# A dilated convolution: the fifth pair's load in two parts, and a small copy ahead of the first store

## The chip, the core and the metric

The kernel runs on one core of a Trainium2 chip. The metric is the device time of one execution in microseconds (us); the kernel before takes 126.56 us (median of 3 runs, 126.45 to 127.11).

The core's engines each run their own instruction stream: TensorE (PE) multiplies, VectorE (DVE), ScalarE (ACT) and GpSimd (POOL) work element by element, and SyncE (SP) issues transfers. Transfers themselves are carried out by 16 DMA engines, which take work from two queues here: SyncE's (f32 to f32) and GpSimd's (which also turns f32 into f16 on the way).

## The reference

```python
batch, c_in, h, w, c_out, k, dilation = 16, 64, 64, 64, 128, 3, 2
x_pad = np.pad(x, ((0, 0), (0, 0), (pad, pad), (pad, pad)), mode='constant')
for b in range(batch):
    for co in range(c_out):
        for ci in range(c_in):
            for kh in range(k):
                for kw in range(k):
                    output[b, co] += weight[co, ci, kh, kw] * x_pad[b, ci, kh*dilation:kh*dilation+h, kw*dilation:kw*dilation+w]
```

A 3 x 3 convolution with dilation 2, 64 channels to 128, on 16 images of 64 x 64, in f32. The input has 16.8 MB, the output 33.6 MB.

## The kernel before

Two images make a pair: their 2 x 64 input channels fill the 128 partitions. There are eight pairs (`NP`), counted pb = 0 to 7, and for each one

- a load of 128 partitions x 4096 values, f32 in memory and f16 in the tile `x16[pb]`. Pair 0 is loaded as f32 by SyncE (line 75) into a buffer of the output pool and converted on the chip; pairs 1 to 7 are loaded by GpSimd (line 81, and line 89 for the last one, which is cut unevenly);
- a sum on GpSimd (`prepare`, line 151): within each group of four rows the first two rows plus the last two, in the tile `s16[pb]`. With it, three products take the place of four;
- four units of 16 output rows (`NU`), each with three phases of matmuls into PSUM (line 196). The first phase works on `s16` and is copied out by ScalarE (line 217); the two others work on `x16`, and VectorE adds that copy to each (line 222) and writes the output tile `o`;
- a store from `o` to memory by SyncE (lines 233 to 237): one DMA of 4 MB for pairs 0 to 4, two of 2 MB for pairs 5 and 6 (pairs from `BOTH` = 5 on go image by image), and four of 1 MB for pair 7.

The order of the work is the order of the code; nothing is moved by a scheduler. Each engine takes its instructions in that order and waits by semaphores where it needs another's result. What matters around the change:

- GpSimd, at the start: the load of pair 1 (line 120), the first piece of pair 0's sum (line 155), the loads of pairs 2, 3 and 4 one right after another (lines 156 and 157, `AHEAD` = 5), and three more pieces of pair 0's sum (lines 158 and 159). Later loads are issued two pairs ahead, from within the loop (lines 205 to 209): pair 5's in pair 3's place of GpSimd's stream, and so on. DMAs of GpSimd's queue are worked off in order on each DMA engine.
- SyncE, at the start: the weight (line 64) and pair 0 in two pieces (line 75). After that it does nothing but the 13 stores, each waiting for VectorE to have finished its tile. A store that waits holds up all behind it on SyncE.
- Output tiles: `opool` has three buffers. `x32`, the f32 copy of pair 0, takes the first, so the tiles of pairs 0, 1, 2 are in the second, third and first one; pair 3 writes where pair 0's tile was and has to wait until that is stored, pair 4 waits for pair 1's, and so on.
- `x16pool` has six buffers, so the loads of pairs 1 to 5 wait for no buffer. `sumpool` has three: pair 4's sum takes the buffer of pair 1's.

Of the kernel before, what the change touches and what calls it, by code (L numbers as in the profile page):

```python
# [10 lines left out]
def kernel(  # L11
# [7 lines left out]
    nc = tc.nc  # L19

    B, CI, H, W = x.shape
# [5 lines left out]
    P = 128  # L27
    f32 = mybir.dt.float32
    f16 = mybir.dt.float16
    NP = B // 2  # L30
# [18 lines left out]
    wpool = ctx.enter_context(tc.tile_pool(name="wpool", bufs=1))  # L49
    x16pool = ctx.enter_context(tc.tile_pool(name="x16pool", bufs=6))  # L50
# [9 lines left out]
    x_pair = x.rearrange("(nb two) c h w -> nb (two c) h w", two=2)  # L60
# [5 lines left out]
    x16 = {}  # L66
# [11 lines left out]
    def load(pb, cuts):  # L78
        x16[pb] = x16pool.tile([P, H, W], f16, tag="x16", name=f"x16_{pb}")
        for lo, hi in zip(cuts, cuts[1:]):  # L80
            nc.gpsimd.dma_start(out=x16[pb][:, lo:hi], in_=x_pair[pb, :, lo:hi])  # L81

    def load_uneven(pb):
        x16[pb] = x16pool.tile([P, H, W], f16, tag="x16", name=f"x16_{pb}")
        cut, p1 = H - 36, P - 16
        parts = [(0, p1, 0, H), (p1, P, 0, cut)]
        parts += [(p, p + 4, cut, H) for p in range(p1, P, 4)]
        for p0, p2, lo, hi in parts:
            nc.gpsimd.dma_start(  # L89
                out=x16[pb][p0:p2, lo:hi], in_=x_pair[pb, p0:p2, lo:hi]  # L90
            )

    AHEAD = 5
# [16 lines left out]
    for name, a in (("w21", 2), ("w01", 0)):  # L110
        for u in range(2):
            eng = nc.vector if name == "w21" else nc.gpsimd
            eng.tensor_sub(  # L113
                out=w16[:, SLOT[name] * KW : (SLOT[name] + 1) * KW, u, :],
# [8 lines left out]
    for n, name in enumerate(("w1", "w21", "w0", "w01", "w2")):  # L123
        ps = cpool.tile([P, 2, NB], f32, tag="ps", name=f"wt{n}")
        k0 = SLOT[name] * KW
        for j in range(KW):
            nc.tensor.matmul(  # L127
                out=ps[:, 0, j * CO : (j + 1) * CO],
# [16 lines left out]
    def prepare(pb, lo, hi):  # L145
        if pb not in s16:
            s16[pb] = sumpool.tile([P, 2 * NQ, W], f16, tag="s16", name=f"s16_{pb}")
        src = (x16[pb] if pb else x32).rearrange("p (q e r) w -> p q e (r w)", e=2, r=2)
        dst = s16[pb].rearrange("p (q r) w -> p q (r w)", r=2)
        q0, q1 = lo // 4, hi // 4  # L150
        nc.gpsimd.tensor_add(  # L151
            out=dst[:, q0:q1], in0=src[:, q0:q1, 0, :], in1=src[:, q0:q1, 1, :]
        )

    prepare(0, 0, 20)
    for pb in range(2, AHEAD):
        load(pb, [0, H])
    for lo, hi in zip(cuts0[1:], cuts0[2:]):
        prepare(0, lo, hi)

# [30 lines left out]
    def phase(pb, u, terms):  # L191

        ps = cpool.tile([CO, 2, NB], f32, tag="ps", name="ps")
        for pair in zip(*(conv(pb, hb, ps[:, hb], u, terms) for hb in range(2))):
            for m in pair:
                nc.tensor.matmul(**m)  # L196
        return ps

    BOTH = NP - 3
    for pb in range(NP):  # L200
        o = opool.tile([P, 2, H, W], f32, tag="o", name=f"o{pb}")
        ov = o.rearrange("p b (q e r) w -> p b q e (r w)", e=2, r=2)
        for u in range(NU):

            if u == 1 and AHEAD <= pb + 2 < NP:
                if pb + 3 == NP:
                    load_uneven(pb + 2)
                else:
                    load(pb + 2, [0, H])
            if pb + 1 < NP:  # L210
                if u == 1:
                    prepare(pb + 1, 0, 36 if pb + 1 < 3 else H)
                elif u == 2 and pb + 1 < 3:
                    prepare(pb + 1, 36, H)

            s32 = spool.tile([P, 2, NB], f32, tag="s32", name="s32")
            nc.scalar.copy(out=s32, in_=phase(pb, u, [("w1", 2, 0)]))  # L217
            for e, terms in enumerate(
                ([("w21", 1, 0), ("w0", 1, -1)], [("w01", 0, 0), ("w2", 0, 1)])
            ):  # L220
                ps = phase(pb, u, terms)
                nc.vector.tensor_add(  # L222
                    out=ov[:, :, u * UQ : (u + 1) * UQ, e, :],
                    in0=ps.rearrange("p b (q c) -> p b q c", c=QW),
                    in1=s32.rearrange("p b (q c) -> p b q c", c=QW),
                )

            step = NU // 2 if pb == NP - 1 else NU  # L230
            if (u + 1) % step == 0:
                fl = slice((u + 1 - step) * 4 * UQ, (u + 1) * 4 * UQ)
                if pb < BOTH:
                    nc.sync.dma_start(out=out_pair[pb], in_=o)
                else:
                    for hb in range(2):
                        nc.sync.dma_start(out=out[2 * pb + hb, :, fl], in_=o[:, hb, fl])
# [35 lines left out]
```

## Time and profile before

| | |
|---|---|
| time, median of 3 runs | 126.56 us (126.45 to 127.11) |
| the profiled execution | 126.83 us, of which the span from the first to the last instruction is 125.1 us |
| granted TensorE clock | 0.965 of full speed, mean of the span |
| TensorE busy | 104.8 us (84% of the span) |
| VectorE busy | 81.9 us (66%) |
| GpSimd busy | 43.0 us (34%) |
| ScalarE busy | 39.6 us (32%) |
| SyncE's DMA queue (weight, pair 0, all stores) | 35.95 MB, 68.4% of the time of 16 DMA engines |
| GpSimd's DMA queue (loads of pairs 1 to 7) | 7.34 MB as written, 28.9% |

The two queues' shares of DMA time add up to 97.3%. A load of GpSimd's queue reads twice the bytes that it writes, and the profile counts those written.

The stores, by their issue on SyncE: 23.43 us (pair 0), 35.80 (pair 1), 48.17 (pair 2), 60.54 (pair 3), 75.59 (pair 4), 87.97 (the first of pair 5) and so on to 113.08 (the last). The five stores of 4 MB take 24.3 us from issue to landing (median), the four of 2 MB 12.5 us; the six loads of 1 MB (as written) 15.3 us.

How to read what the prediction shows: times are microseconds from the start of the span. A row of the timeline has the start, the duration, the engine, the line of the kernel, the operation with the tiles that it writes and reads, the count, and in brackets the engine's idle time before it and what ended that. "SPq" is SyncE's issuing of a DMA, not the transfer. In the rows of "slices" the span is cut into 40 equal parts of 3.13 us; the digit of the DMA row is the busy share of the 16 DMA engines in tenths (9 is 90% or more).

### The profile page before, as it was taken

What the parts mean: (1) busy time and instruction counts of PE and PEld (TensorE: products, weight loads), DVE (VectorE), ACT (ScalarE), POOL (GpSimd) and SP (SyncE); (2) the same over time, 40 slices, a digit from 0 to 9 for tenths busy, and PEclk for the clock granted to TensorE, in tenths of its full rate; (3) what the DMA queues carried; (4) which work ended last, traced back from release to release, by engine and by line L of the source; (5) the groups of instructions that cost most, each with busy time, mean ns of one, the idle gap of its engine ahead of it and who ended that gap; (6) DMA issues with size and microseconds to landing.
All of it is one profiled execution on the core that took longest, in us unless ns stands there. A gap on an engine that the chain in (4) does not pass through costs nothing.

```text
span 125.1 us, 2248 instructions
## 1 busy us (share of the span) xinstructions
PE 104.8 (84%) x981; PEld 56.0 (45%) x981; DVE 81.9 (66%) x71; ACT 39.6 (32%) x40; POOL 43.0 (34%) x33
## 2 busy tenths in 40 slices
PE   6379999999999999999947999999999999960000
PEld 2055555555555555555524555555555555520000
DVE  0484877877787778777319978777877787770000
ACT  4777333333333333333330333333332433310000
POOL 2789696993580079507500093000000000000000
PEclk9999999999999999999999999999999999999655
DMA  4999999999999999999999999999999999999991
GB/s 138 368 332 210 212 215 220 220 170 367 375 330 309 343 299 333 335 301 333 330 420 410 422 435 435 424 440 419 419 425 445 430 422 435 425 417 409 432 406 76
DMA packets 4105, 43.42 MB, mean 347 GB/s; under 512 B 496, under 2 KB 496, under 8 KB 784
## 3 DMA queue, kind: packets, MB, share of 16 engines
q1 hardware_dynamic: 2944, 35.95, 68.4%
q0 software_dynamic: 1152, 7.34, 28.9%
q8 instruction: 7, 0.11, 0.3%
q14 instruction: 2, 0.02, 0.0%
HBM read 17.07 MB, written 33.55 MB: 405 GB/s over the span
## 4 chain that ended last, share of the span: by engine, by line
PE 55%; DMA 28%; DVE 4%; POOL 1%; DVEq 1%; issue 0%; SPq 0%
PE ps L196 55%; DMA out_dram<-o 24%; DMA x<-in_x_dram 5%; DVE o L222 4%; POOL s L151 1%; DVEq L268 1%; SPq L64 0%; DVEq L222 0%
## 5 line engine op out<-in xcount | busy, mean ns | idle before, releaser
L222 DVE TENSOR_TENSOR o<-ps,s 128x1024 f32<-128x1024 f32 x64 | 76.7, 1222 | 25.9 <-PE ps L196 17.1
L196 PE MATMUL ps<-x,w_sb 64*128 64x496 f16 (+3 forms) x768 | 84.9, 366 | 2.5 <-DVE o L222 2.5
L196 PEld LDWEIGHTS <-w_sb 64*128 64x128 f16 x960 | 53.7, 94 | 49.6 <-issue 4.8
L217 ACT COPY s<-ps 128x1024 f32<-128x1024 f32 x32 | 32.4, 1012 | 66.9 <-PE ps L196 66.9
L151 POOL TENSOR_TENSOR s<-x 128x2048 f16<-128x2048 f16 (+5 forms) x13 | 33.8, 2616 | 30.0 <-PE ps L196 23.6
L196 PE MATMUL ps<-s,w_sb 64*128 64x496 f16 (+1 forms) x192 | 26.6, 379 | 0.7 <-POOL s L151 0.7
L81 POOL DMA_DIRECT2D x<-in_x_dram x6 | 3.8, 634 | 0.0
L103 PE MATMUL warm<-zero 128*128 128x512 f16 x6 | 2.7, 630 | 1.2 <-DVE zero L97 1.2
L127 PE MATMUL wt<-ident,w 128*128 128x128 f16 x15 | 1.8, 312 | 2.1 <-ACT w L109 2.1
L113 DVE TENSOR_TENSOR w<-w 128x192 f16<-128x192 f32 x2 | 1.5, 796 | 2.5 <-DMA w<-in_weight_dram 2.5
L89 POOL DMA_DIRECT2D x<-in_x_dram x6 | 3.1, 522 | 0.0
L127 PEld LDWEIGHTS <-w 128*128 128x128 f16 x15 | 1.5, 145 | 3.1 <-ACT w L109 3.1
L109 ACT CAST w<-w 128x576 f16<-128x576 f32 x2 | 2.3, 1222 | 1.7 <-DMA w<-in_weight_dram 1.7
L142 ACT CAST x<-x 128x1024 f16<-128x1024 f32 (+1 forms) x3 | 2.8, 975 | 0.1
L113 POOL TENSOR_TENSOR w<-w 128x192 f16<-128x192 f32 x2 | 1.9, 956 | 2.4 <-DMA w<-in_weight_dram 2.4
L136 DVE CAST w_sb<-wt 128x384 f16<-128x384 f32 x3 | 1.6, 547 | 1.4 <-PE wt L127 1.4
L140 DVE CAST x<-x 128x1280 f16<-128x1280 f32 x1 | 2.1, 2057 | 0.0
L103 PEld LDWEIGHTS <-zero 128*128 128x128 f16 x6 | 0.7, 138 | 2.3 <-DVE zero L97 1.2
L109 ACT ACT_TABLE_LOAD x1 | 1.3, 1283 | 0.7 <-PEq L254 0.7
L138 ACT CAST w_sb<-wt 128x384 f16<-128x384 f32 x2 | 1.0, 479 | 1.1 <-PE wt L127 1.1
L97 DVE MEMSET zero<- 128x256 uint32 x1 | 0.3, 272 | 0.9 <-PEq L254 0.9
masks.py:199 POOL TENSOR_SCALAR_AFFINE_SELECT ident<-ident 128x128 f16<-128x128 f16 x1 | 0.3, 295 | 0.1
(5 smaller groups left out, 0.6 us busy)
## 6 DMA issues: line engine op xcount, KB each, us to landing
out_dram<-o SPq DMA_DIRECT2D x5, 4096.0 KB, 24.3
out_dram<-o SPq DMA_DIRECT2D x4, 2048.0 KB, 12.5
x<-in_x_dram POOLq DMA_DIRECT2D x6, 1024.0 KB, 15.3
out_dram<-o SPq DMA_DIRECT2D x4, 1024.0 KB, 10.7
x<-in_x_dram SPq DMA_DIRECT2D x1, 1152.0 KB, 5.7
x<-in_x_dram SPq DMA_DIRECT2D x1, 896.0 KB, 7.4
x<-in_x_dram POOLq DMA_DIRECT2D x1, 896.0 KB, 15.2
w<-in_weight_dram SPq DMA_DIRECT2D x1, 288.0 KB, 2.9
```

Source lines behind the costliest of these rows:

```text
L81: nc.gpsimd.dma_start(out=x16[pb][:, lo:hi], in_=x_pair[pb, :, lo:hi])
L89: nc.gpsimd.dma_start(out=x16[pb][p0:p2, lo:hi], in_=x_pair[pb, p0:p2, lo:hi])
L103: nc.tensor.matmul(out=warm[:, 0], lhsT=zero[:, 0:P], rhs=zero, start=True, stop=True)
L109: nc.scalar.copy(out=w16[:, 0:NK, u, :], in_=w32k)
L113: eng.tensor_sub(out=w16[:, SLOT[name] * KW : (SLOT[name] + 1) * KW, u, :], in0=w32k[:, a * KW : (a + 1) * KW, :], in1=w32k[:, KW : 2 * KW ...
L127: nc.tensor.matmul(out=ps[:, 0, j * CO : (j + 1) * CO], lhsT=w16[:, k0 + j, :, :].rearrange("o t i -> o (t i)"), rhs=ident, start=True, st ...
L140: nc.vector.tensor_copy(out=x16[0][:, 0:20], in_=x32[:, 0:20])
L142: nc.scalar.copy(out=x16[0][:, lo:hi], in_=x32[:, lo:hi])
L151: nc.gpsimd.tensor_add(out=dst[:, q0:q1], in0=src[:, q0:q1, 0, :], in1=src[:, q0:q1, 1, :])
L196: nc.tensor.matmul(**m)
L217: nc.scalar.copy(out=s32, in_=phase(pb, u, [("w1", 2, 0)]))
L222: nc.vector.tensor_add(out=ov[:, :, u * UQ : (u + 1) * UQ, e, :], in0=ps.rearrange("p b (q c) -> p b q c", c=QW), in1=s32.rearrange("p b ( ...
```

## The change

Pair 4, the last of the loads that are issued before the loop, is taken out of the loop of loads and written out: its tile is made as before, and two GpSimd DMAs fill it, the first with partitions 0 to 31 (a quarter, 512 KB of f32), the second with partitions 32 to 127. They stand where the one load stood, behind those of pairs 2 and 3.

Ahead of pair 0's store, SyncE is given a DMA of its own: it copies the first row of partition 0 of that tile (64 values of f16, 128 bytes) into a new tile `gate`, which nothing reads. The copy reads what the first of the two loads writes, so SyncE waits for this one to land, and for the second one it does not wait; in the built program the copy is cut into 16 pieces of 8 bytes. The first store stands behind it on SyncE.

`BOTH` goes from 5 to 6: pair 5 is stored by one DMA of 4 MB in place of two of 2 MB. SyncE's DMAs thus stay 16 in number.

```diff
     prepare(0, 0, 20)
-    for pb in range(2, AHEAD):
+    for pb in range(2, AHEAD - 1):
         load(pb, [0, H])
+    last = AHEAD - 1
+    x16[last] = x16pool.tile([P, H, W], f16, tag="x16", name=f"x16_{last}")
+    for p0, p1 in ((0, 32), (32, P)):
+        nc.gpsimd.dma_start(out=x16[last][p0:p1], in_=x_pair[last, p0:p1])
     for lo, hi in zip(cuts0[1:], cuts0[2:]):
         prepare(0, lo, hi)
...
-    BOTH = NP - 3
+    BOTH = NP - 2
     for pb in range(NP):
...
             if (u + 1) % step == 0:
                 fl = slice((u + 1 - step) * 4 * UQ, (u + 1) * 4 * UQ)
+                if pb == 0:
+                    gate = wpool.tile([1, W], f16, name="gate")
+                    nc.sync.dma_start(out=gate, in_=x16[last][0:1, 0])
                 if pb < BOTH:
                     nc.sync.dma_start(out=out_pair[pb], in_=o)
```

Matmuls, additions, copies and the instructions of TensorE, VectorE and ScalarE are the same ones in the same order.

## The prediction, made before the changed kernel was run

> **What bounds the kernel now.** I read the page's slices first, then the byte counts, then the chain, then what the stores' queue waits for at the end.
>
> ```profile
> DMA  4999999999999999999999999999999999999991
> GB/s 138 368 332 210 212 215 220 220 170 367 375 330 309 343 299 333 335 301 333 330 420 410 422 435 435 424 440 419 419 425 445 430 422 435 425 417 409 432 406 76
> HBM read 17.07 MB, written 33.55 MB: 405 GB/s over the span
> PE ps L196 55%; DMA out_dram<-o 24%; DMA x<-in_x_dram 5%; DVE o L222 4%; POOL s L151 1%; DVEq L268 1%; SPq L64 0%; DVEq L222 0%
> ```
>
> The DMA engines are busy in every slice but the first and the last. The GB/s row needs a key: a GpSimd load turns f32 into f16 and is counted by the f16 it writes, so 214 there is 428 of memory traffic, the same as the 420 to 445 of the slices with stores alone. Counted so, the engines run at one speed, about 430, all the way; 50.6 MB at 430 are 117.7 us of the 125.1. One slice stands out: the ninth, 25.0 to 28.1 us, at 170 after 220 and before 367. The stage is looked at closer here (columns: stretch, its length, granted clock, DMA share, GB/s):
>
> ```profile
> 20.00:25.20 5.20, 1.00 1.03 214
> 25.20:27.50 2.30, 1.00 1.04 153
> 27.50:30.00 2.50, 1.00 0.98 315
> 70.00:112.00 42.00, 1.00 1.01 428
> ```
>
> The next answers say who is behind it. Pair 0's store is issued at 23.43 us; the loads of pairs 3 and 4 are then in the queue (issued at 9.3 and 9.8).
>
> ```profile
> 23.43 12.76 SPq L234 DMA_DIRECT2D out_dram<-o  x2
> ...
> 24.70 4.07 POOL L151 TENSOR_TENSOR s<-x 128x2048 f16<-128x2048 f16 x1 [0.19 <-DMA x<-in_x_dram]
> 28.72 0.57 POOL L81 DMA_DIRECT2D x<-in_x_dram  x1
> 32.56 4.06 POOL L151 TENSOR_TENSOR s<-x 128x2048 f16<-128x2048 f16 x1 [3.26 <-DMA x<-in_x_dram]
> ```
>
> GpSimd's sum of pair 3 starts at 24.70, when x3 has landed; that of pair 4 waits until 32.56 for x4. So from 25.2 to 27.5 only x4 moves, at 153 in place of 214: 2.30 x (1 - 153/214) = 0.66 us of all engines is lost. It begins 1.8 us after the first store's issue, while a load is under way, and no later slice shows the like. I take it as the price of the first store's coming into engines full of loads.
>
> The rest of the kernel has room:
>
> ```profile
> 65.31 2.36 DVE L222 TENSOR_TENSOR o<-ps,s 128x1024 f32<-128x1024 f32 x2 [4.80 <-DMA out_dram<-o]
> 112.00:121.00 9.00, 0.74 1.01 426
> SPq L268 <- DMA out_dram<-o: 9.4, 4, 2.4
> ```
>
> VectorE stands 4.80 us at 65.31 for pair 1's store (35.80, 29.4 us to landing), and TensorE 2.5 us behind it; this is how the chain, followed back, comes to lie on TensorE (55%) for the most part. But the last store is issued at 113.1 and lands 11.1 us later, though its 1 MB takes 2.5 us at 428, and the engines move 426 GB/s to the end: 8.6 us of other stores and start-up lie ahead of it. If up to 4.1 of these are start-up (below), compute has some 4.5 us to spare at the end. Transfers set the time.
>
> **The change part by part.** Sums go against the profiled execution: span 125.1 us, 126.83 in all, 0.27 above the median of 126.56.
>
> *Two loads for one, on GpSimd.* One more issue of 0.50 to 0.57 us (rows of L81 and L89; 0.86 at most) at 10.3 us. Behind it on GpSimd stand pair 0's three remaining sums (10.34, 3.48 us, so 1.16 each). The first would end at 12.1 instead of 11.5; TensorE reads it at 12.52. The next needs to be there at 15.69. Pair 1's sum waits for x1 until 14.87 anyhow and GpSimd is done at 14.4. Price 0; without that cover, 0.4 us at most, inside the 4.5 of the end. The bytes are the same. Whether 32 partitions load as fast per byte as 128 is not shown in a run of loads alone; the nearest rows are the 112- and 16-partition loads of L89, 15.2 us to landing against 15.3 for full ones. I take 0, bounds 0 and 0.3 us (a quarter of a load taking a quarter longer).
>
> *The wait on SyncE.* A load of 1.05 MB in f16 at 214 GB/s takes 4.9 us. x3 lands at about 24.6, x4's first quarter 1.2 us later, 25.8. Then the small copy is issued (0.37 us, the shortest store issue), and pair 0's store at about 26.2 instead of 23.43: 2.8 us later. Behind it on SyncE only pair 1's store waits, issued at 35.80, so nothing else is held up. Who waits for pair 0's store: pair 3 writes the same buffer, first at 48.63; it lands at 23.4 + 23.1 = 46.5, so 2.1 us are spare. Were the whole 2.8 us to reach that landing, VectorE would stand 0.7 us. But x4, no longer sharing, is done near 29 instead of near 30.5 to 32.4, and the store then has the engines to itself until x5 (issued at 28.72, flowing from 33: the GB/s of 30 to 33 is 418). So I count nothing here.
>
> *The small copy.* 128 bytes, in 16 pieces. No row has its like; below, its issue alone (0.37 us, counted above), above, as much as one of the 18 KB loads adds, 1.2 us to its neighbour's landing, though on SyncE's queue nothing waits for it. I take 0.
>
> *x4 sooner.* GpSimd's sum of pair 4 needs the buffer of pair 1's sum, which TensorE reads last at 31.23 + 0.81 = 32.04. So it starts at 32.1 instead of 32.56 and the issue of x6 (36.58) moves up 0.5 us, behind x5 in the queue. 0.
>
> *Pair 5's store in one.* One issue of some 0.45 us less on SyncE at 88, where DMA is at 428 GB/s and the queue has a backlog (4 MB stores land 18.9 us and more after their issue). 0, bounds 0.05 either way. SyncE still issues 16 DMAs, and the last stores' semaphores were last used by pairs 0 to 3, long landed.
>
> *The dip.* The store's 1.8 us of start-up now ends at 28.0, when x4, alone at full speed, has 24.6 + 4.9 = 29.5 as its last landing and most engines are done a little before. So the store should come into engines that are just running empty. I take most of the 0.66 back, 0.55; bounds: all of it (0.66), and, if the engines stand idle for the store, a loss worked out under the rivals.
>
> Sum: 125.1 - 0.55 = 124.55 of span, 126.3 for that execution, 126.0 against the median.
>
> **The rivals.**
> *A, the forecast:* the dip goes, 126.0; its own range is 125.7 to 126.35.
> *B, the dip belongs to the store and moves with it.* For: stores of a fresh queue may start slowly by themselves; the loads at the beginning also do, 347 GB/s from 2 to 5 us against 407 from 5 to 8. Against: in the dip the loads slow down, which a store waiting by itself would not do. 0.66 lost at 28 instead of 25: no change, 126.4 to 126.8.
> *C, the engines run empty.* GB/s rises only at 27.5, 4.1 us after the store's issue. If that is the store's own delay, and not its turn behind loads, it flows from 26.2 + 4.1 = 30.3, and engines that finished x4 between 28.6 and 29.5 stand 0.8 to 1.7 us. Less the dip's 0.66: +0.15 to +1.0, middle 127.1. It decides as soon as the start-up with empty engines is over some 3 us. Against: the first load of all (weight) has landed 2.9 us after its issue, with 288 KB (0.7 us) moved.
> *D, a load in two pieces pays a fixed price twice,* and opens the gate late. From rows: x2 and x3 land at about 20.2 and 24.5, 4.3 us apart, less than the 4.9 of x3's bytes, so queued loads show none. Above, the weight's 2.9 us less 0.7 of bytes and less about 1 us of start: 1.2 us. The gate then opens at 27.0, the store is issued at 27.4 and flows between 29.2 and 31.5 (1.8 to 4.1 later), and the engines, done at 29.0 on the mean, stand 0.2 to 2.5 us. Less the dip's 0.66: 126.1 to 128.4, middle 127.2. The Trainium skill, "DMA: Bandwidth & Descriptors", section "Anatomy of one DMA — SWDGE (gpsimd) path", puts a fixed cost of about 2.0 us on each such DMA, most of it between the last byte and the semaphore, and its "Rules for kernel authors" advise against cutting a transfer by partitions; by that the gate would open near 27.8 and the time be near 128. The 4.3 us between x2 and x3 do not show it between queued loads, and no row has a small load alone.
>
> **How the numbers follow.** A 0.50, B 0.26, C 0.17, D 0.07. A measurement of this kernel can tell about 0.5% (0.63 us) from no change: faster is below 125.93, slower above 127.19. A needs nearly the whole dip to be faster: half of it (0.25), and B's edge 0.01. Slower: C 0.15 and D 0.05, and 0.02 for a price not seen. The range goes from 125.5 (all of the dip, and 0.4 of scatter: the runs before lie 0.66 apart) to 127.4, past the middle of C and D.
>
> **What would show it.** The first store's issue at about 26.2, behind a small copy at 25.8. No slice under 210 before GB/s jumps, and the jump at 28 to 29; a dip of the same depth there is B, a slice in which the DMA share falls below 0.9 is C, a gate after 26.5 is D. x4 landed by 29.5 to 30 (GpSimd's sum of pair 4 at 32.1). Pair 0's store landed before 48.6, VectorE's stall at 65 down by about half a us, and the last landing as much earlier. I am wrong if the whole of x4 is waited for (store issued at 29 or later), or if the dip's time was never one of the store.

## The result, and the profile after

| | before | after |
|---|---|---|
| time, median of 22 runs each | 126.19 us (125.83 to 127.61) | 127.19 us (126.56 to 129.02) |
| ratio | | 1.0069, 95% interval 1.0044 to 1.0095 |
| the profiled execution | 126.83 us | 126.94 us |
| its span | 125.1 us | 124.9 us |
| its time outside the span | 1.8 us | 2.05 us |

The change makes the kernel slower, by 0.7% as the ratio has it; 126.0 was forecast. The two profiled executions hide this: the one of before took 0.64 us more than its kernel's median, the one of after 0.25 less. One of the 22 executions after, that of 129.02 us, was a slow one and is not in the ratio.

The page of after, the slices:

```profile
DMA  5999999999999999999999999999999999999991
GB/s 138 354 347 218 228 213 213 213 241 417 357 325 341 336 315 317 323 386 299 302 368 406 429 411 425 430 430 430 415 451 430 425 407 420 451 404 422 428 394 47
```

The timeline of after around the first store, GpSimd's and SyncE's rows:

```profile
24.48 4.07 POOL L151 TENSOR_TENSOR s<-x 128x2048 f16<-128x2048 f16 x1 [1.23 <-DMA x<-in_x_dram]
28.49 0.56 POOL L81 DMA_DIRECT2D x<-in_x_dram  x1
34.88 4.07 POOL L151 TENSOR_TENSOR s<-x 128x2048 f16<-128x2048 f16 x1 [5.83 <-PE ps L200]
```

```profile
25.57 0.59 SPq L239 DMA_DIRECT2D gate<-x  x1
26.20 12.67 SPq L241 DMA_DIRECT2D out_dram<-o  x2
```

The same stage by stretches (stretch, length, granted clock, DMA share, GB/s):

```profile
20.00:25.20 5.20, 1.00 1.00 208
25.20:27.50 2.30, 1.00 1.09 228
27.50:30.00 2.50, 1.00 0.97 387
30.00:33.00 3.00, 1.00 1.04 437
33.00:35.00 2.00, 1.00 0.95 283
...
70.00:112.00 42.00, 1.00 1.00 426
```

The wait works as meant: the copy is issued at 25.57 and the store at 26.20. The dip is gone, the ninth slice has 241 in place of 170 and the stretch from 25.2 to 27.5 has 228 in place of 153. x4's second part lands at 29.24. So the forecast's first half happened. But the stretch from 33 to 35, in which x5, the load of pair 5, begins to come in, has 283. Loads and stores are mixed there and a load counts half; from the trace's packets (its records of what each DMA engine moved), a load's counted by the f32 that it reads, it is 346 GB/s of memory traffic in the microsecond from 33 and 388 in the next, where before had 427 and 426.

From here on, "loss" is this: memory traffic so counted, microsecond by microsecond of the trace, as far as it is below 430 GB/s, added up from 24 to 40 us and divided by 430. (The expectations call such a microsecond a "second", and they count the pairs from one: their fifth pair is pair 4 with the load x4, their sixth pair 5 with x5.) It is 0.81 us in the profile of before and 0.39 in that of after.

Compute is not what holds the end. Chain and SyncE's waits of after:

```profile
9.33 100.91 PE ps L200 x948
```

```profile
SPq L239 <- DMA x<-in_x_dram: 23.5, 1, 23.5
...
SPq L275 <- DMA out_dram<-o: 9.2, 4, 2.4
```

VectorE's stall of 4.80 us at 65 is gone, so the chain runs through TensorE without a break, but the last store is issued at 113.10 (before: 113.08) and the end waits 9.2 us for stores, as before it waited 9.4.

### The profile page after: what moved, and what is told of

Read it like the earlier page. It is cut to its first block, busy times and chain, and to the rows that moved or that the text cites. A ratio compares the mean times of both kernels' runs of the same rounds, so it can differ in the third digit from the quotient of the medians.

```text
span 124.9 us, 2252 instructions
## 1 busy us (share of the span) xinstructions
PE 106.5 (85%) x981; PEld 55.6 (44%) x981; DVE 81.0 (65%) x71; ACT 39.6 (32%) x40; POOL 43.7 (35%) x34
## 4 chain that ended last, share of the span: by engine, by line
PE 81%; DMA 5%; POOL 2%; DVE 1%; DVEq 1%; SPq 0%; issue 0%
PE ps L200 81%; DMA x<-in_x_dram 5%; POOL s L151 2%; DVE o L226 1%; DVEq L275 1%; SPq L64 0%; DVEq L226 0%
## 5 line engine op out<-in xcount | busy, mean ns | idle before, releaser
L200 PE MATMUL ps<-x,w_sb 64*128 64x496 f16 (+3 forms) x768 | 86.5, 372 | 0.0
L151 POOL TENSOR_TENSOR s<-x 128x2048 f16<-128x2048 f16 (+5 forms) x13 | 34.3, 2657 | 32.3 <-PE ps L200 30.2
L140 DVE CAST x<-x 128x1280 f16<-128x1280 f32 x1 | 0.8, 815 | 0.0
## 6 DMA issues: line engine op xcount, KB each, us to landing
x<-in_x_dram POOLq DMA_DIRECT2D x1, 896.0 KB, 15.1
```

The lines of the kernel that those rows point to most:

```text
L151: nc.gpsimd.tensor_add(out=dst[:, q0:q1], in0=src[:, q0:q1, 0, :], in1=src[:, q0:q1, 1, :])
```

## The experiments

Each kernel below starts from the kernel before or from the changed one; "span" is the median over an experiment's timed executions where there are several.

**The kernel before, again.** No edit.

> The kernel before, unchanged, to see its span, the time outside the span and a second profile of the first store. Theory 1 (the first store collides with the loads in every execution, and the loss of 0.66 us is regular): a slice of about 153 GB/s again 1.8 us after the first store's issue, span 124.4 to 125.1 us. Theory 2 (the collision in the first profile was one execution's bad luck): no stretch under 200 GB/s before GB/s jumps, and a span near 124.4. Theory 3 (part of the loss by the change lies outside the span): time minus span is 1.7 to 1.8 us here against the 2.05 us of the changed kernel's runs; otherwise 2.05 here too. Ratio 1.000.

Ratio 1.0016 (0.9993 to 1.0039). The median span is 124.4 us, the time outside it 1.80. Its first store and the stretches:

```profile
25.05 12.76 SPq L234 DMA_DIRECT2D out_dram<-o  x2
```

```profile
25.20:27.50 2.30, 1.00 1.07 221
27.50:30.00 2.50, 1.00 1.00 403
30.00:33.00 3.00, 1.00 1.01 431
33.00:35.00 2.00, 1.00 0.98 311
```

221 where the first profile had 153: this is the same kernel, and there is no dip. Its store was issued at 25.05 instead of 23.43, and it loses 0.14 us instead of 0.81. Theory 1 falls: the loss is not regular. It is not the bad luck of one execution alone either, as theory 2 has it; three more profiles below, with an early first store, lose 0.25 to 0.53 us. Theory 3 holds: part of the change's loss, 0.25 us, lies outside the span.

Why the same kernel issues its first store at different times is seen in TensorE's first rows, here of the first profile of before and then of this one:

```profile
8.53 1.44 PE L196 MATMUL ps<-s,w_sb 64*128 64x512 f16 x6 [0.66 <-POOL s L151]
9.73 2.96 PE L196 MATMUL ps<-x,w_sb 64*128 64x512 f16 x24
```

```profile
9.29 1.44 PE L196 MATMUL ps<-s,w_sb 64*128 64x512 f16 x6 [1.49 <-POOL s L151]
10.50 3.82 PE L196 MATMUL ps<-x,w_sb 64*128 64x512 f16 x24
```

The 24 matmuls take 2.96 us in one and 3.82 in the other; each takes 0.51 to 0.63 us up to 10.2 us in the first and up to 12.7 in the second (14.9 in the profile of after, where the 24 take 4.85), and 0.32 to 0.38 later. The start of pair 0 is 0.8 us later and slow for longer, and pair 0 is stored that much later.

**The parts of the change, one at a time.** The split alone:

```diff
-    for pb in range(2, AHEAD):
+    for pb in range(2, AHEAD - 1):
         load(pb, [0, H])
+    last = AHEAD - 1
+    x16[last] = x16pool.tile([P, H, W], f16, tag="x16", name=f"x16_{last}")
+    for p0, p1 in ((0, 32), (32, P)):
+        nc.gpsimd.dma_start(out=x16[last][p0:p1], in_=x_pair[last, p0:p1])
```

> The fifth pair's load in 32 and 96 partitions; no small copy, and the fifth and sixth pairs stored as before. Theory 1 or 2 with the loss made by the later store: ratio 0.998 to 1.002. Theory 4 (the second issue on GpSimd, 0.52 us, or the split loads themselves cost): ratio 1.004 to 1.009, and TensorE's matmuls of pair 0 start later than 8.6 us.

1.0020 (0.9998 to 1.0042), span 124.4, outside 2.06. All that the split costs lies outside the span. Pair 5 stored by one DMA, alone:

```diff
-    BOTH = NP - 3
+    BOTH = NP - 2
```

> The sixth pair stored by one DMA of 4 MB in place of two of 2 MB, nothing else changed. All theories but one: ratio 0.998 to 1.002. Theory 5 (the order of rows in the one large store leaves the DMA engines less even at the end): ratio 1.003 to 1.007, with the last landings further apart than the 2.5 us of before.

1.0011 (0.9988 to 1.0034), span 124.5: nothing. Split and copy without that edit (`BOTH` left at `NP - 3`):

> The split load and the small copy, the sixth pair stored in two DMAs as before. If the later store is what costs: ratio 1.004 to 1.009 as for the whole change, the first store issued at about 26.2. If the single store of the sixth pair costs (theory 5): ratio 0.995 to 1.002 here.

1.0127 (1.0109 to 1.0145) in four executions, span 125.65; the profile's store at 26.30, loss 0.66. The loss comes with the copy and its wait. It is larger than expected and larger than that of the whole change (1.0069); why is not shown.

**The copy without the wait.**

```diff
-                    nc.sync.dma_start(out=gate, in_=x16[last][0:1, 0])
+                    nc.sync.dma_start(out=gate, in_=x16[1][0:1, 0])
```

> The whole change, but the small copy reads pair 1's tile, which has landed by 15 us, so that SyncE does not hold the first store back. Theory 6 (the held-back store costs: GpSimd's queue has run empty when the sixth load comes, at 33 us, into engines full of stores, and there 0.25 to 0.5 us are lost): span back at 124.4 to 124.5, no second under 405 GB/s of memory traffic at 33 to 35 us, ratio 1.002 by what lies outside the span alone. Theory 7 (the small copy or the split by themselves do it, the wait doesn't matter): span 125.0 to 125.6, ratio 1.006 to 1.012. Time outside the span 2.05 us in either.

1.0011 (0.9979 to 1.0043), span 124.4: the time is that of before, so neither copy nor split costs in the span. The expected clean profile did not come, though: the profiled execution was a long one (125.0), it has 348 and 347 GB/s at 33 and 34 us, and its store came at 26.37 by itself, since TensorE was slow until 15.1. A late store thus shows the dip at 33 without being held back.

**Waiting for the whole load**, in one piece (an excerpt; `BOTH` is `NP - 2` as in the change):

```diff
+                if pb == 0:
+                    gate = wpool.tile([1, W], f16, name="gate")
+                    nc.sync.dma_start(out=gate, in_=x16[AHEAD - 1][0:1, 0])
                 if pb < BOTH:
```

> The fifth pair's load in one piece again, the small copy waiting for all of it, the sixth pair's store in one. Time outside the span back at 1.80 us. By theory 6 the store is issued at about 29.5 to 30.5, the engines stand empty for 1 to 2 us before it, and the sixth load still comes into stores alone at 33: span 125.5 to 126.5, ratio 1.008 to 1.016. By theory 7 with the split as the cause: span 124.4, ratio 1.000; with the small copy as the cause: 125.0 to 125.6.

1.0245 (1.0211 to 1.0279), more than expected; store at 30.07, span 127.9, outside 1.83. The stretches:

```profile
27.50:30.00 2.50, 1.00 0.14 23
30.00:33.00 3.00, 1.00 1.02 161
33.00:35.00 2.00, 1.00 1.11 180
```

The DMA engines stand nearly empty from 28 to 30 us; the share from 27.5 to 30 is 0.14. What flows first after that is not the store but x5: issued at 28.69, it has its first packet at 29.96. The store, issued at 30.07, has its first one at 35.72, among those of x5. So x5 does not come into stores alone here, as theory 6 had it; the store comes into x5. Counted by the f32 that is read, the loads move 159 GB/s in the microsecond from 30 and 428 in that from 32, and the traffic falls once more, to 244 from 35, before the store flows. Loss 3.89 us.

**Later without any copy.** VectorE fills an unused tile ahead of pair 0's last addition:

```diff
                 ps = phase(pb, u, terms)
+                if pb == 0 and u == NU - 1 and e == 1:
+                    pause = wpool.tile([P, 1024], f32, name="pause")
+                    nc.vector.memset(pause, 0.0)
```

> The kernel before, but VectorE fills an unused tile of 128 x 1024 f32 (about 1.1 us) ahead of pair 0's last addition, so that the first store is issued some 1.1 us later, at 26.1 to 27.0 in place of 25.0 to 25.9 in the usual execution; no small copy, no split load. Theory 6 (an issue from about 26.2 on costs 0.4 to 0.7 us, whatever brings it): span 124.9 to 125.3, ratio 1.003 to 1.007, two seconds under 400 GB/s at 33 to 35 us. Theory 8 (the small copy in SyncE's queue makes that dip; all three profiles that show it have the copy): span 124.4, ratio 1.000, no dip.

1.0043 (1.0008 to 1.0077), span 125.2 against 124.4. The profiled execution was one of the short ones (124.6), store at 26.02, no dip. So the time speaks for theory 6, and the profile, of an execution without the loss, cannot say. Two longer fills, one execution each, show it.

> As with the fill of 128 x 1024, but 128 x 2048 (about 2.2 us): first store at 27.0 to 28.1, no copy, no split load. Theory 6: 1 to 2 us lost between 24 and 40 us, seconds under 350 GB/s among them, span 125.4 to 126.4. Theory 8 (the copy does it): at most 0.5 us lost, by engines that stand empty at 28 us alone, and no second under 405 GB/s at 33 to 35.

> The same with a fill of 128 x 1408 (about 1.5 us): first store at 26.5 to 27.4. Theory 6: 0.5 to 1.3 us lost between 24 and 40 us, a second under 400 GB/s at 33 to 35. Theory 8: under 0.3 us, none.

Stores at 28.02 and 28.86, losses 1.97 and 2.29, spans 126.4 and 127.1. The second is later and loses more than expected: pair 0 itself came late in that execution. The first one's store and stretches:

```profile
28.02 10.69 SPq L237 DMA_DIRECT2D out_dram<-o  x2
```

```profile
27.50:30.00 2.50, 1.00 0.58 226
30.00:33.00 3.00, 1.00 1.13 437
33.00:35.00 2.00, 1.00 0.86 184
```

Engines partly empty from 27.5 to 30 (share 0.58) and then the dip at 33, deeper than with the change, and no copy in the program. Theory 8 falls.

**Waiting for less.** The copy waits for the fourth pair's load (x3), none is split; the edit is shown against the kernel that waits for the whole load:

```diff
-                    nc.sync.dma_start(out=gate, in_=x16[AHEAD - 1][0:1, 0])
+                    nc.sync.dma_start(out=gate, in_=x16[AHEAD - 2][0:1, 0])
```

> The small copy waits for the fourth pair's load (landed at 24.3 to 24.8 in all profiles) in place of part of the fifth's; no load is split; the sixth pair's store in one. The first store is then issued at 24.8 to 25.0 at the earliest. Theory 6: only the executions in which the store would come at 23.4 are changed, span 124.2 to 124.5, ratio 0.997 to 1.001. Theory 8: the dip at 33 us is there, span 125.0, ratio 1.005.

0.9994 (0.9970 to 1.0018), span 124.3; in 11 of 12 executions it is at most 124.5, one has 125.8. Copy at 24.52, store at 25.57, loss 0.08. The copy and a wait do no harm where they don't make the store late; nor is this faster than before by anything that these runs can tell. This kernel is the nearest to the forecast's own term: the store no longer comes in before x3 has landed, and it is not late.

The fifth pair's load in four parts of 32, the copy waiting for the first of them:

> The change with the fifth pair's load in four parts of 32 partitions, the small copy waiting for the first. Time outside the span 1.80 us as with four parts before. Theory 6: first store at 26.2 or later in every execution, span 125.0 to 125.4 as with the change, ratio 1.004 to 1.007. If the split in 32 and 96 were what makes the span longer: span 124.4, ratio 1.000.

1.0060 (1.0038 to 1.0082), span 125.15, outside 1.83; store at 26.72, loss 0.94. In four parts of 16, 32, 32 and 48:

> The change, but the fifth pair's load in 16, 32, 32 and 48 partitions, the small copy waiting for the first 16: 0.6 us earlier than the change. Theory 6: the first store issued at 25.4 to 25.9 in the usual execution, which the profiles without a wait show to be harmless; span 124.3 to 124.7, ratio 0.998 to 1.002, no second under 400 GB/s between 24 and 40 us. If waiting for a part of this load is bad in itself: span 125.1, ratio 1.005. Time outside the span 1.80 us (15 loads).

1.0093 (1.0067 to 1.0119). This one missed its aim: the fourth pair landed at 25.05 in the profile, the first 16 partitions 0.9 us after it and not 0.6, and the store was issued at 26.57, past the harmless stretch; loss 1.09. Half of that, 0.54 us, lies at 28 to 30 us, where the store comes in among the last loads, with the engines busy (share 1.09 from 28 to 29). It does not test what it was made for. The copy waiting for the second of four parts of 32:

> Four parts of 32, the small copy waiting for the second: first store at about 27.6 to 27.9. Theory 6: the loss between 24 and 40 us is larger than the 0.4 to 0.9 us of issues at 26.2 to 26.7 and smaller than the 3.9 us of an issue at 30.1: 1 to 2 us, span 125.5 to 126.3.

Store at 27.83, loss 1.92, span 126.4, a little above the expected.

**All profiles by the first store's issue** (us, the loss from the packets as above; the split alone and those below without a copy are among them):

| issue | loss | kernel | issue | loss | kernel |
|---|---|---|---|---|---|
| 23.43 | 0.81 | before | 25.87 | 0.06 | sixth pair in one |
| 24.18 | 0.53 | 13 loads otherwise | 26.02 | 0.13 | fill of 1024 |
| 24.48 | 0.43 | halves | 26.20 | 0.39 | the change |
| 24.75 | 0.25 | three parts | 26.30 | 0.66 | split and copy |
| 25.05 | 0.14 | before, again | 26.37 | 0.49 | copy, no wait |
| 25.24 | 0.19 | split alone | 26.57 | 1.09 | 16 partitions |
| 25.57 | 0.08 | wait for x3 | 26.72 | 0.94 | wait, four parts |
| 25.74 | 0.12 | four parts | 27.83 | 1.92 | wait for second |
| 25.76 | 0.15 | seven loads | 28.02 | 1.97 | fill of 2048 |

At 28.86 and 30.07 it is 2.29 and 3.89. Below 25 most of the loss lies at 24 to 29 us, where the store comes in among loads. From 26.20 to 28.86 most or much of it lies at 33 to 36, where x5 comes in among stores, and from 27.83 on also at 28 to 30, where the engines are partly empty; the 16 partitions and the wait for the whole load (30.07) differ from this as said above. Each row is one execution, and the moment alone does not set the size: at 26.37 and 26.57 it is 0.49 and 1.09.

**The time outside the span.** Five kernels, one execution each, none with a copy. The fifth pair's load in four parts of 32:

> The fifth pair's load in four parts of 32 partitions, no small copy, 15 GpSimd loads in place of 12. If each further load adds to the time outside the span: 1.8 + 3 x 0.25 = 2.55 us outside. If there is a step between 12 and 13 loads: 2.05 us. If the 32 partitions do it, whatever their number: 2.05 us.

The last pair's load in one:

> The last pair's load in one piece in place of six, 7 GpSimd loads in place of 12. If each load counts: 1.8 - 5 x 0.25 = 0.55 us outside the span. If only a step at 13: 1.80 us. The span is not compared, since this also takes the uneven sharing of the last load away.

The fifth pair's in 64 and 64:

> The fifth pair's load in 64 and 64 partitions, no small copy; 13 GpSimd loads as in the change. If the 96 partitions bring the 0.25 us outside the span: 1.80 us outside. If 13 loads do: 2.05 us.

In 32, 32 and 64:

> The fifth pair's load in 32, 32 and 64 partitions, no small copy: 14 GpSimd loads. If an odd one out at 13 is what costs: 1.80 us outside the span; if 13 and 14 do: 2.05 us.

In four of 32, with the last pair's small pieces joined to two:

> The fifth pair's load in four parts of 32, the last pair's four small pieces joined into two: 13 GpSimd loads cut in another way, no small copy. If the number 13 does it: 2.05 us outside the span. If it is the two parts of the fifth pair's load: 1.80 us.

Time of the profiled execution less its span, by the number of GpSimd loads: 7: 1.77; 12: 1.77 to 1.80 in eight profiles; 13: 2.02 to 2.06 in six kernels, cut in three ways; 14: 2.17; 15: 1.79 to 1.81 in four. It goes with the number and not with the shape (15 are cut in two ways), but neither guess fits: it is no price per load and no step. What it is stays open.

## Why the prediction was wrong, point by point

- **"Transfers set the time", and compute has some 4.5 us to spare.** Right as to the transfers; the 4.5 was not tested. TensorE was late by 2.7 us for pairs 1 to 3 in the profile of after (second store at 38.50 instead of 35.80), the stall at 65 went altogether (half a us less was expected), and the last store was issued at the same 113.1.
- **Two loads for one: 0.** Right in the span (124.4 with the split alone). Outside the span it costs 0.25 us, a term that the sum did not have: it was made against the profiled execution's own 1.8 us of such time, taken as given.
- **The wait on SyncE: the copy at 25.8, the store at 26.2.** 25.57 and 26.20. x4's last landing 29.24 against 29.5, pair 0's store landed at 44.53, before 46.5 and before the 48.6 at which it is needed.
- **Pair 5's store in one: 0.** 1.0011 (0.9988 to 1.0034).
- **The dip: "I take most of the 0.66 back, 0.55".** This step failed. The 0.66 was read off one execution, in which pair 0 was done early, at 23.43. In eight other profiles of kernels without a wait or a fill it was issued at 24.18 to 25.87 (in a ninth, the copy without a wait, at 26.37), and in the five of these at 25.05 or after the loss is 0.06 to 0.19 us, in the three earlier ones 0.25 to 0.53: in most executions there was little or next to nothing to take back. The kernel that waits for x3 alone had the early executions' collision out of the way without being late, and its time is 0.9994 (0.9970 to 1.0018) of before: some 0.1 us gained, 0.38 at most, where 0.55 was counted on. The profile's own time, 0.27 us above the median of three then known and 0.64 above the later one, was the hint; I noted it and used the 0.66 as if every execution had it.
- **The same step, its other side.** "Comes into engines that are just running empty" was right at 28 us: no microsecond from 24 to 33 is below 420 in the profile of after. But a price came up at 33 to 35 us, where x5 meets the stores, which no rival had. The prediction had seen x5 flow from 33 and put the later store at nothing ("So I count nothing here"), because it asked only who waits for its landing. The gate opens when x4's first part has landed, and in the three profiles with a gate on 32 partitions the store is at 26.20, 26.30 and 26.72, the rising side of the table; an execution in which it would have come at 25 to 26 is moved there as well.
- **Rival B**, the dip moves with the store, gave a time near that of before. A dip did come back, but elsewhere, and not where the store starts. **Rival C** had the sign and a time (127.1) close to what was measured, but not the mechanism: there are no empty engines in the profile of after, and the store's own start is nearer 1 us than 4.1: with the engines partly empty, in the kernel with the fill of 2048, the store issued at 28.02 has its first packet at 28.94. The time before a store's first packet is no fixed one: 4.1 us in the first profile of before, 1.5 in that of after, 5.65 in the kernel that waits for the whole load. **Rival D**, a fixed price for the first part of the load, falls: the part landed 1.25 us after x3, its bytes' time. The Trainium skill, "DMA: Bandwidth & Descriptors", section "Anatomy of one DMA — SWDGE (gpsimd) path", puts about 2.0 us of fixed cost on each such DMA; this trace shows none of it between queued loads. That 127.19 lies among the times of C and D is luck: neither mechanism is seen in the profile of after.

The sum with what was measured: +0.25 us outside the span, and 0.7 in the span (125.1 against 124.4, medians). Of the latter, the profile of after against that of before, again, shows 0.25 more loss from 24 to 40 us and 0.1 from 40 to 80; most of the rest is at the end, where the 16 DMA engines finish a little less evenly (the last packet 1.6 us after their mean, against 1.2). Together the last store lands at 123.99 against 123.28. How much of this unevenness is the change's is not shown: the kernel with the sixth pair in one had it too, in an execution of 125.0 with no dip.

What stays open is why x5 costs traffic at 33 to 35 us after a late first store and not after one at 25 to 26; the issue of that load is at 28.5 to 29.4 in either, except where pair 0 itself came late (29.82). That the late store is the cause is shown: with the same copy the time is that of before where the store is not held back (1.0011 and 0.9994) and longer where it is (1.0060 to 1.0245), and a fill on VectorE without any copy makes it longer too (1.0043, at least 1.0008). That a slow start of pair 0 does the same rests on one profile (26.37).

## What to carry to other kernels

A loss that is read from one profiled execution is a loss of that execution: before pricing its removal, ask what set its moment, and whether the other executions share it; a profile slower than its kernel's median is the one to doubt. A gate that opens at a fixed point of the transfers does not only hold back the early executions, it moves the others there too, and the stretch between too early and too late was about 1 us wide in these profiles. In a kernel with full DMA engines, count what lies outside the span too.

## What the hardware showed that was not expected

- The first store's moment has a best stretch: 0.06 to 0.19 us lost at 25.05 to 26.02, 0.81 at 23.43 and 0.39 to 1.09 at 26.20 to 26.72.
- In a dip the DMA engines are not idle; the packets of the queue that is already running take longer, in the microsecond or so before the newcomer's first packet. In the first profile of before a load's packet of 16 KB of f32 takes 1155 ns (median of those that start from 26 to 27 us) in place of 625, and the store's first packet starts at 27.55. In the profile of after a store's packet of 16 KB takes 881 ns from 33 to 34 in place of 611, and 1208 with the fill of 2048; x5's first packets start at 33.76 and 34.59. Why is not shown.
- A change in the number of GpSimd loads moved the time outside the span: 1.8 us with 7, 12 and 15, 2.05 with 13, 2.17 with 14.
- TensorE's first matmuls of pair 0 run at little over half speed for a time that differs between executions, while the profile grants the full clock. Stretches of the first profile of before and of after (stretch, length, busy time and number of TensorE's instructions, granted clock, DMA share, GB/s):

```profile
8.50:10.20 1.70, 1.68 (x10) 1.00 1.08 207
10.60:16.00 5.40, 5.40 (x56) 1.00 1.03 215
```

```profile
9.30:14.90 5.60, 5.57 (x30) 1.00 1.02 214
15.20:20.00 4.80, 4.80 (x48) 1.00 1.05 218
```

Ten matmuls in 1.70 us and 30 in 5.60, against 56 in 5.40 and 48 in 4.80, so 0.17 and 0.19 us each against 0.10. The Trainium skill, "TensorE: Matmul & The Clock Gate", Part 1, has the array start at half its clock until it has been busy for a window of some 3.4 us; the halving agrees roughly, and the end of it came 1.7 us after pair 0's first matmul in one execution and 5.5 us after it in the other.
